# A pre-norm's variances and gain products placed on GpSimd, in a hybrid encoder layer on one core

## The chip, the core and the metric

The kernel runs on one core of a Trainium2 chip. A core has engines that each work through an instruction queue of their own, in order, and wait for each other by semaphores: TensorE (PE, with PEld for its weight loads), VectorE (DVE), ScalarE (ACT), GpSimd (POOL) and SyncE (SP, which here issues all the DMAs). SBUF is the on-chip memory of 128 partitions, PSUM the accumulators that PE writes. The metric is the device time of one execution in microseconds. Before the change it is 1018.42 us, the median of 3 runs (1018.4 to 1018.56).

## The reference

One layer over 1024 tokens of width 1024, all in float32. The input is normed, projected by one large matrix, and the parts of the projection go through three branches (causal pooling, short convolution, stick-breaking attention) whose gated results are projected, summed, projected again, normed and added to the input:

```python
def rms_norm(x, g):
    xf = x.astype(jnp.float32)
    y = xf * lax.rsqrt(jnp.mean(xf * xf, axis=-1, keepdims=True) + RMS_EPS)
    return (y * g.astype(jnp.float32)).astype(x.dtype)

def hybrid_layer(x, g_pre, w_in, pool_w, pool_scale, conv_w, conv_b, w_branch, w_out, g_post):
    h = rms_norm(x, g_pre)
    u = jnp.einsum('bsd,dn->bsn', h, w_in)
    ...
    return x + rms_norm(out, g_post)
```

Only the first line of the layer, the pre-norm h, concerns the change: per token the mean of the squares, plus RMS_EPS = 1e-6, to the power of -0.5, times the token's row, times g.

## The kernel before

**Precision and layout.** Every float32 operand of a matrix product is split into a high part (a rounded copy) and a low part (the rest), and each product is three products of PE: high by high, high by low, low by high. The high part is a cast on ACT, the low part a subtraction on DVE or POOL (`split`, lines 72 to 74: tiles w_hi, w_lo, q_w). The normed input is kept transposed, as hh (high) and hl (low): for each half of the model dimension (0 or 1, four blocks of 128 rows) and each half of the tokens (0 to 511, 512 to 1023). In the listings below, hh_0_70 and hl_0_74 belong to the first half of the tokens and half 0 of the model dimension, hh_0_72 and hl_0_76 to the first half of the tokens and half 1; hh_1_71 with hl_1_75 and hh_1_73 with hl_1_77 are the same two for the second half of the tokens.

**The pre-norm.** The tokens come in eight blocks of 128 (tile xt, 128 x 1024, eight buffers, loaded by line 267). `normed(i)` (lines 270 to 279) does for block i: on ACT the squares with their sum per token (tile ssq, line 274; a result row for the sum stands behind it as ACTIVATION_READ_ACCUMULATOR), on DVE the variance (tile var, line 276), on POOL its power of -0.5 (tile rstd, line 278), on DVE the product of row, rstd and g in place (line 279). g_bc is g, loaded once onto all partitions. `transposed(i)` (lines 281 to 291) then transposes the block on PE into a PSUM tile, four 128 x 128 pieces for each half of the model dimension, and splits it: ACT casts to hh (line 290), DVE subtracts to hl (line 291). The PSUM tiles xtp are four buffers, two for each block, so the transposes of a block reuse the buffers of the block two before it, once hh and hl of that block are written.

**The first products.** K and Q of the first head pair are computed while the norms go on (lines 319 to 326): for each half of the tokens, first K (three products for each of eight steps, `half_block`), then Q. In Q's first half the transposes of blocks 4 to 7 stand behind every second step. Each of the two results of K and Q sits in one of two PSUM banks (g_ps), and K's second half reuses the bank of K's first half, which `k_parts` (lines 237 to 248) empties: ACT copies it to khi (line 244), DVE subtracts to klo (line 245), ACT copies both to the other half of the partitions (lines 246 and 247), for two sides, one after the other. Q's weights (q_w) are split with their low part on POOL.

**What sets the order.** The program is written in a straight line, and the framework places instructions into the queues of the engines by its own estimate of when each is ready; so a moved instruction can change the order of its neighbours on every engine. SP's queue is not reordered by this change. The weights w_raw go through three buffers; a load into a buffer waits for the splits of the one before.

Of the kernel before, what the change touches and what calls it, by code (L numbers as in the profile page):

```python
# [11 lines left out]
ALU = mybir.AluOpType  # L12
# [3 lines left out]
D = 1024  # L16
# [5 lines left out]
EPS = 1e-6  # L22
# [13 lines left out]
def hybrid_block_kernel(ctx, tc, x, g_pre, w_in, pool_w, pool_scale, conv_w, conv_b, w_branch, w_out, g_post, out):  # L36
# [12 lines left out]
    nc = tc.nc  # L49
    op = lambda name, bufs, **kw: ctx.enter_context(tc.tile_pool(name=name, bufs=bufs, **kw))  # L50
# [210 lines left out]
    with tc.tile_pool(name="xp", bufs=1) as xp, tc.tile_pool(name="ps_s", bufs=2, space=PSUM) as ps_s:  # L261
        g_bc = xp.tile([P, D], F32, tag="g", name="g_bc")
# [7 lines left out]
        def normed(i):  # L270
            xt = xns[i]
            junk = xp.tile([P, D], F32, tag="junk", name="junk")
            ssq = xp.tile([P, 1], F32, tag="ssq", name="ssq", bufs=4)
            nc.scalar.activation(junk, xt, AF.Square, accum_out=ssq)
            var = xp.tile([P, 1], F32, tag="var", name="var", bufs=4)
            nc.vector.tensor_scalar(out=var, in0=ssq, scalar1=1.0 / D, scalar2=EPS, op0=ALU.mult, op1=ALU.add)
            r = xp.tile([P, 1], F32, tag="rstd", name="rstd", bufs=4)
            nc.gpsimd.tensor_tensor(out=r, in0=var, in1=expo[:, 0:1], op=ALU.pow)
            nc.vector.scalar_tensor_tensor(out=xt, in0=xt, scalar=r, in1=g_bc, op0=ALU.mult, op1=ALU.mult)

        def transposed(i):

# [16 lines left out]
        for i in range(2):  # L299
            normed(i)  # L300
# [3 lines left out]
        for i in range(2, 4):  # L304
            normed(i)
# [4 lines left out]
        for i in range(4, 8):  # L310
            normed(i)
# [25 lines left out]
    with tc.tile_pool(name="wt", bufs=3) as wtp, \  # L337
# [106 lines left out]
        for n in range(len(steps) + LAG + 1):  # L444
            if n < len(steps):
                p, s, i = steps[n]
# [371 lines left out]
    def square(ps, var):  # L818
        ssq = fin.tile([P, 1], F32, tag="ssq", name="ssq", bufs=4)
        nc.scalar.activation(junk[:, 0:ps.shape[-1]], ps, AF.Square, accum_out=ssq)  # L820
        o = fin.tile([P, 1], F32, tag="var", name="var", bufs=S // P + 4)
        if var is None:
            nc.vector.tensor_scalar(out=o, in0=ssq, scalar1=1.0 / D, scalar2=EPS, op0=ALU.mult, op1=ALU.add)
        else:
            nc.vector.scalar_tensor_tensor(out=o, in0=ssq, scalar=1.0 / D, in1=var, op0=ALU.mult, op1=ALU.add)
        return o
# [26 lines left out]
    for i in range(n_tok):  # L853
# [4 lines left out]
        var = kept_var[i]  # L858
        pieces = (slice(0, HALF),) if i < n_tok - 1 else (slice(0, 256), slice(256, HALF))
        for es in pieces:  # L860
            ps = out_bank()[:, 0:es.stop - es.start]
            out_products(i, ps, range(KB), 1, es)
            var = square(ps, var)
            scaled(ps, o1[:, es], slice(HALF + es.start, HALF + es.stop))
        r = fin.tile([P, 1], F32, tag="rstd", name="rstd", bufs=2)
# [45 lines left out]
```

## Time and profile before

| what | before |
|---|---|
| median of 3 runs | 1018.42 us |
| the profiled execution itself | 1018.75 us |
| its span, first to last instruction | 1017.0 us |
| mean granted TensorE clock | 0.994 |
| busy DVE / ACT / POOL | 632.2 / 447.2 / 448.3 us |
| end of block 3's sum of squares, start of its norm on DVE | 11.27, 16.46 us |

A line of the order of time reads: start and duration in us, engine, line of the kernel, operation, output<-inputs, shape, count, and in brackets how long the engine stood idle before it and what ended that. Groups and single lines of the program are given as durations in nanoseconds (min/median/max) with the start of the first and the last. The tables by stretch of time give, for each stretch, its length, then the busy time of PE, PEld, DVE, ACT and POOL with their counts, the granted TensorE clock (1.00 is full speed), the busy share of the DMA engines and what they moved in GB/s.

The profile in 40 equal slices shows where the pre-norm lies, in the first two slices of 25 us each:

```profile
PE   5999999999998999999999999999999999999997
...
POOL 3034443644565015445455554445555565655000
```

PE's first digit is 5: it waits for about half of the first slice. Behind that it is busy in nearly every slice.

### The profile page before, as it was taken

Reading aid. Unit: us, or ns where it says so; the run is one execution under the profiler, and the core shown is the slowest. Engines: PE = TensorE matmul, PEld = TensorE weight load, DVE = VectorE, ACT = ScalarE, POOL = GpSimd, SP = SyncE. Lnnn points to the kernel's source line nnn. Section 1 sums busy time; section 2 is a strip of 40 time slices with the busy share of each in tenths; the row PEclk is TensorE's granted clock in tenths of the full one; section 3 lists DMA queues with packets and bytes.
Section 4 is the critical chain, followed back from the end, with each engine's and each line's share of the span. In section 5 each row is a group of like instructions: output and inputs, shape, how many; then the busy total and the mean of one; then the engine's idle time right before and its main releaser. Section 6 shows DMA issues by size and latency. Waiting matters only on the chain.

```text
span 1017.0 us, 13273 instructions
## 1 busy us (share of the span) xinstructions
PE 989.9 (97%) x4752; PEld 829.1 (82%) x4752; DVE 632.2 (62%) x847; ACT 447.2 (44%) x871; POOL 448.3 (44%) x359
## 2 busy tenths in 40 slices
PE   5999999999998999999999999999999999999997
PEld 4788888888887888887888888888888888888886
DVE  6556776767776978899776776556333443464233
ACT  7557668658665553332222223343322422353111
POOL 3034443644565015445455554445555565655000
PEclk8999999999999999999999999999999999999999
DMA  6101000100101441222212224455433633166033
GB/s 240 51 22 33 31 22 22 42 21 22 32 23 32 165 156 62 92 75 68 80 61 68 79 72 164 150 195 175 135 124 124 217 121 111 61 201 222 1 125 125
DMA packets 43986, 97.09 MB, mean 95 GB/s; under 512 B 5264, under 2 KB 5520, under 8 KB 43920
## 3 DMA queue, kind: packets, MB, share of 16 engines
q1 hardware_dynamic: 43920, 96.24, 29.2%
q8 instruction: 38, 0.62, 0.3%
q14 instruction: 28, 0.23, 0.1%
HBM read 73.15 MB, written 23.07 MB: 95 GB/s over the span
## 4 chain that ended last, share of the span: by engine, by line
PE 89%; ACT 4%; DVE 3%; POOL 2%; issue 1%; DMA 1%; SPq 0%; POOLq 0%; DVEq 0%; ACTq 0%
PE q_ps L555 26%; PE g_ps L555 18%; PE g_ps L190 14%; PE pp L507 13%; PE o_ps L809 8%; PE o L434 3%; PE tp L420 2%; DVE sn L402 1%; PE z L398 1%; PE z L395 1%; ACT sn L399 1%; POOL sp L404 1%; POOL w_lo L74 1%; DMA g_bc<-in_pre_norm_g_dram 1%; ACT sp L400 1%
## 5 line engine op out<-in xcount | busy, mean ns | idle before, releaser
L74 POOL TENSOR_TENSOR w_lo<-s,w_hi 128x512 fp32r<-128x512 f32 x95 | 132.0, 1391 | 176.0 <-ACT w_hi L73 172.5
L404 POOL TENSOR_TENSOR sp<-sp,sn 128x127 f32<-128x127 f32 (+3 forms) x64 | 80.5, 1260 | 131.3 <-DVE sn L402 66.2
L74 POOL TENSOR_TENSOR w_lo<-s_raw,w_hi 128x512 fp32r<-128x512 f32 x70 | 94.9, 1355 | 93.3 <-ACT w_hi L73 89.6
L402 DVE TENSOR_TENSOR_SCAN sn<-sn,zeros 128x128 f32<-128x128 f32 (+3 forms) x64 | 101.9, 1592 | 46.3 <-ACT sn L399 41.6
L73 ACT CAST w_hi<-s 128x512 fp32r<-128x512 f32 x96 | 59.6, 621 | 131.4 <-PE q_ps L555 62.3
L190 PE MATMUL g_ps<-hh,w_hi 128*128 128x512 f32 x240 | 100.9, 420 | 0.3 <-ACT hh L290 0.3
L73 ACT CAST w_hi<-s_raw 128x512 fp32r<-128x512 f32 x70 | 43.5, 622 | 128.5 <-PE q_ps L555 62.2
L190 PE MATMUL g_ps<-hl,w_hi 128*128 128x512 f32 x240 | 95.2, 397 | 0.5 <-DVE hl L291 0.5
L190 PE MATMUL g_ps<-hh,w_lo 128*128 128x512 f32 x240 | 95.3, 397 | 0.0
L74 POOL TENSOR_TENSOR w_lo<-w_raw,w_hi 128x512 fp32r<-128x512 f32 x44 | 67.0, 1523 | 52.7 <-ACT w_hi L73 49.7
L555 PE MATMUL q_ps<-hh,w_lo 128*128 128x512 f32 x224 | 87.2, 389 | 0.7 <-POOL w_lo L74 0.7
L555 PE MATMUL q_ps<-hl,w_hi 128*128 128x512 f32 x224 | 87.2, 389 | 0.0
L555 PE MATMUL q_ps<-hh,w_hi 128*128 128x512 f32 x224 | 87.2, 389 | 0.0
L507 PE MATMUL pp<-yhi,w_lo 128*128 128x512 f32 x192 | 74.7, 389 | 0.0
L507 PE MATMUL pp<-ylo,w_hi 128*128 128x512 f32 x192 | 74.7, 389 | 0.0
L507 PE MATMUL pp<-yhi,w_hi 128*128 128x512 f32 x192 | 74.7, 389 | 0.0
L555 PE MATMUL g_ps<-hh,w_hi 128*128 128x512 f32 x160 | 62.3, 389 | 0.0
L555 PE MATMUL g_ps<-hl,w_hi 128*128 128x512 f32 x160 | 62.3, 389 | 0.0
L555 PE MATMUL g_ps<-hh,w_lo 128*128 128x512 f32 x160 | 62.2, 389 | 0.0
L399 ACT ACTIVATE sn<-z 128x384 f32<-128x384 f32 (+2 forms) x96 | 48.0, 500 | 28.3 <-PE z L398 17.8
L235 DVE TENSOR_TENSOR wl<-tp,wh 128x512 fp32r<-128x512 f32 (+2 forms) x96 | 50.2, 543 | 14.1 <-ACT wh L421 13.4
L421 ACT CAST wh<-tp 128x512 fp32r<-128x512 f32 (+2 forms) x96 | 44.9, 495 | 20.6 <-PE tp L420 15.2
(205 smaller groups left out, 2412.8 us busy)
## 6 DMA issues: line engine op xcount, KB each, us to landing
s_raw<-in_w_in_dram SPq DMA_DIRECT2D x96, 256.0 KB, 2.6
pr<-proj SPq DMA_DIRECT2D x48, 256.0 KB, 3.5
proj<-g SPq DMA_DIRECT2D x20, 512.0 KB, 3.0
w_raw<-in_w_in_dram SPq DMA_DIRECT2D x34, 256.0 KB, 2.6
w_raw<-in_w_branch_dram SPq DMA_DIRECT2D x24, 256.0 KB, 2.7
xt<-in_x_dram SPq DMA_DIRECT2D x8, 512.0 KB, 7.9
proj<-proj SPq DMA_DIRECT2D x8, 512.0 KB, 3.0
wo_raw<-in_w_out_dram SPq DMA_DIRECT2D x16, 256.0 KB, 3.2
```

What stands on the lines that cost most here:

```text
L73: nc.scalar.copy(hi, raw)
L74: eng.tensor_tensor(out=lo, in0=raw, in1=f32(hi), op=ALU.subtract)
L190: nc.tensor.matmul(ps, l[:, a], r[k // 4][t][:, k % 4, :], start=(n == 0), stop=(n == 3 * KB - 1))
L235: nc.vector.tensor_tensor(out=o, in0=a, in1=f32(b), op=ALU.subtract)
L399: nc.scalar.activation(sn[:, c0:c1], z[:, :w], AF.Sigmoid, scale=-0.125)
L402: nc.vector.tensor_tensor_scan(out=rev, data0=rev, data1=zeros.to_broadcast([P, n]), initial=1.0, op0=ALU.mult, op1=ALU.max)
L404: nc.gpsimd.tensor_tensor(out=sp[:, 0:n - 1], in0=sp[:, 0:n - 1], in1=sn[:, 1:n], op=ALU.mult)
L421: nc.scalar.copy(wh[c][:, 0:m, qsub], tp[:, 0:m, :])
L434: nc.tensor.matmul(o[:, cs], vc[:, j, s, :], wt[j // 4][:, j % 4, cs], start=(j == 0 and wt is wl), stop=(j == i and wt is wh))
L507: nc.tensor.matmul(pp, l[:, a], r[:, HALVES[t]], start=(n == 0), stop=(n == 3 * NB - 1))
L555: nc.tensor.matmul(bank, l[:, a], r[:, j, :], start=(n == 0), stop=(n == 11))
L809: nc.tensor.matmul(ps, l[:, a], r[:, es], start=(d == 0 and n == 0), stop=(d == KB - 1 and n == 2))
```

## The change

The variance of every block moves from DVE to POOL, right ahead of POOL's power. For the blocks 0 to 3 the product stays as it was. For the blocks 4 to 7 it becomes two instructions: POOL multiplies the raw row by g, in place, and DVE multiplies by rstd, a number for each token.

```diff
             var = xp.tile([P, 1], F32, tag="var", name="var", bufs=4)
-            nc.vector.tensor_scalar(out=var, in0=ssq, scalar1=1.0 / D, scalar2=EPS, op0=ALU.mult, op1=ALU.add)
+            nc.gpsimd.tensor_scalar(out=var, in0=ssq, scalar1=1.0 / D, scalar2=EPS, op0=ALU.mult, op1=ALU.add)
             r = xp.tile([P, 1], F32, tag="rstd", name="rstd", bufs=4)
             nc.gpsimd.tensor_tensor(out=r, in0=var, in1=expo[:, 0:1], op=ALU.pow)
-            nc.vector.scalar_tensor_tensor(out=xt, in0=xt, scalar=r, in1=g_bc, op0=ALU.mult, op1=ALU.mult)
+            if i < 4:
+                nc.vector.scalar_tensor_tensor(out=xt, in0=xt, scalar=r, in1=g_bc, op0=ALU.mult, op1=ALU.mult)
+            else:
+                nc.gpsimd.tensor_tensor(out=xt, in0=xt, in1=g_bc, op=ALU.mult)
+                nc.vector.tensor_scalar(out=xt, in0=xt, scalar1=r, scalar2=None, op0=ALU.mult)
```

Line numbers behind line 279 grow by four (L291 becomes L295). Past the first 45 us no queue changes its order.

POOL's queue before, from the last constant to the first weight split of the next stage:

```order
L170 AFFINE_SELECT future<-future 128x128
L278 TENSOR_TENSOR rstd<-var,expo 128x1 x6
L74 TENSOR_TENSOR q_w<-w_raw,q_w 128x512 x2
L278 TENSOR_TENSOR rstd<-var,expo 128x1 x2
L74 TENSOR_TENSOR w_lo<-w_raw,w_hi 128x512
```

The same place now, from block 5's variance on (block 4's three instructions stand ahead of it in the same order):

```order
L276 TENSOR_SCALAR var<-ssq 128x1
L282 TENSOR_TENSOR xt<-xt,g_bc 128x1024
L278 TENSOR_TENSOR rstd<-var,expo 128x1
L276 TENSOR_SCALAR var<-ssq 128x1
L282 TENSOR_TENSOR xt<-xt,g_bc 128x1024
L278 TENSOR_TENSOR rstd<-var,expo 128x1
L74 TENSOR_TENSOR q_w<-w_raw,q_w 128x512
L276 TENSOR_SCALAR var<-ssq 128x1
L282 TENSOR_TENSOR xt<-xt,g_bc 128x1024
L278 TENSOR_TENSOR rstd<-var,expo 128x1
L74 TENSOR_TENSOR q_w<-w_raw,q_w 128x512
L74 TENSOR_TENSOR w_lo<-w_raw,w_hi 128x512
```

The power of a block now stands behind that block's product, and the two splits of q_w, which stood ahead of the powers of blocks 6 and 7, stand on either side of block 7.

DVE's queue before, from the norm of block 5 to the splits of blocks 4 to 7 (hl_1):

```order
L279 SCALAR_TENSOR_TENSOR xt<-xt,rstd,g_bc 128x1024
L276 TENSOR_SCALAR var<-ssq 128x1 x2
L291 TENSOR_TENSOR hl_1_75<-xtp,hh_1_71 128x4x128
L279 SCALAR_TENSOR_TENSOR xt<-xt,rstd,g_bc 128x1024 x2
L74 TENSOR_TENSOR w_lo<-w_raw,w_hi 128x512
L235 TENSOR_TENSOR klo<-g_ps,khi 64x512 x2
L291 TENSOR_TENSOR hl_1_77<-xtp,hh_1_73 128x4x128
```

And now, from the four norms of blocks 0 to 3 to the same splits:

```order
L280 SCALAR_TENSOR_TENSOR xt<-xt,rstd,g_bc 128x1024 x4
L295 TENSOR_TENSOR hl_0_74<-xtp,hh_0_70 128x4x128 x2
L295 TENSOR_TENSOR hl_0_76<-xtp,hh_0_72 128x4x128 x2
L74 TENSOR_TENSOR w_lo<-w_raw,w_hi 128x512 x2
L295 TENSOR_TENSOR hl_0_74<-xtp,hh_0_70 128x4x128
L295 TENSOR_TENSOR hl_0_76<-xtp,hh_0_72 128x4x128
L295 TENSOR_TENSOR hl_0_74<-xtp,hh_0_70 128x4x128
L295 TENSOR_TENSOR hl_0_76<-xtp,hh_0_72 128x4x128
L283 TENSOR_SCALAR xt<-xt,rstd 128x1024 x4
L74 TENSOR_TENSOR w_lo<-w_raw,w_hi 128x512
L235 TENSOR_TENSOR klo<-g_ps,khi 64x512 x2
L295 TENSOR_TENSOR hl_1_75<-xtp,hh_1_71 128x4x128
```

The four scalings of blocks 4 to 7 now stand in one piece, behind all splits of blocks 0 to 3 and ahead of the weight split, both klo and the first split of block 4, which stood ahead of the norms of blocks 6 and 7. On ACT the squares of block 5 moved behind the four casts of blocks 2 and 3, and the casts of block 4 behind the first cast khi of line 246. On PE the first six transposes of block 4, which stood behind the first product of K, join the other two inside Q's first half.

## The prediction

> **What bounds the kernel now.** First the page: the share of each engine, and the chain that ended last.
>
> ```profile
> PE 989.9 (97%) x4752; PEld 829.1 (82%) x4752; DVE 632.2 (62%) x847; ACT 447.2 (44%) x871; POOL 448.3 (44%) x359
> ...
> PE 89%; ACT 4%; DVE 3%; POOL 2%; issue 1%; DMA 1%; SPq 0%; POOLq 0%; DVEq 0%; ACTq 0%
> ```
>
> PE is busy for 97% and carries 89% of the chain, so the pre-norm can cost or save only what PE waits for it, and PE's work behind it follows back to back: a shift of PE's start is a shift of the end. Next, the order of time on PE for the first 40 us, where the pre-norm lies (tile xtp: transposes of normed tokens; g_ps: the products of the first K and Q blocks).
>
> ```profile
> 17.89 1.94 PE L288 MATMUL xtp<-ident,xt 128*128 128x128 f32 x8 [3.14 <-DVE xt L279]
> ...
> 21.73 0.78 PE L190 MATMUL g_ps<-hl,w_hi 128*128 128x512 f32 x1
> ...
> 33.57 1.03 PE L288 MATMUL xtp<-ident,xt 128*128 128x128 f32 x8
> ...
> 38.11 0.50 PE L190 MATMUL g_ps<-hl,w_hi 128*128 128x512 f32 x1 [0.47 <-DVE hl L291]
> ...
> 38.11 15.07 PE g_ps L190 x65
> ```
>
> Two gates count. **Gate 1**: tokens 0 to 511 are split and the products run from 21.73. **Gate 2**: tokens 512 to 1023 are split and the products of the second half run from 38.11; by the last row, from the chain in order of time, PE then runs 15.07 us without a wait. What the change does to the end is what it does to gate 2. The rows of ACT and DVE ahead of it:
>
> ```profile
> 28.53 0.58 ACT L244 CAST khi<-g_ps 64x512 fp32r<-64x512 f32 x1 [5.00 <-PE g_ps L190]
> 29.86 0.58 ACT L246 CAST khi<-g_ps 64x512 fp32r<-64x512 f32 x1 [0.75 <-DVE klo L235]
> ...
> 31.58 1.08 ACT L290 CAST hh<-xtp 128x512 fp32r<-128x512 f32 x2
> ...
> 36.03 0.58 ACT L257 CAST qa<-g_ps 64x512 fp32r<-64x512 f32 x1 [0.55 <-PE g_ps L190]
> ...
> 25.74 2.48 DVE L279 SCALAR_TENSOR_TENSOR xt<-xt,rstd,g_bc 128x1024 f32<-128x1024 f32 x2 [2.01 <-POOL rstd L278]
> 28.14 0.68 DVE L74 TENSOR_TENSOR w_lo<-w_raw,w_hi 128x512 fp32r<-128x512 f32 x1
> 29.14 0.68 DVE L235 TENSOR_TENSOR klo<-g_ps,khi 64x512 fp32r<-64x512 f32 x1 [0.32 <-ACT khi L244]
> ```
>
> The last two norms, one weight split and the first klo stand in that order on DVE. ACT's second khi waits for that klo, and the casts hh of blocks 4 to 7 queue on ACT behind it. From klo's start to gate 2 it takes 38.11 - 29.14 = 8.97 us.
>
> **The change, part by part.**
>
> *Removed from DVE*: eight variances and, for blocks 4 to 7, the product of three operands. *Added*: a one-input instruction of DVE there, and on POOL eight variances and four products of 128x1024. The prices (duration rows give min/median/max in ns):
>
> ```profile
> L276 DVE TENSOR_SCALAR var<-ssq x8: 143/146/154, 5.7 to 22.8; 128x1 f32<-128x1 f32 x8
> ...
> L279 DVE SCALAR_TENSOR_TENSOR xt<-xt,rstd,g_bc x8: 1276/1284/1286, 7.6 to 26.9; 128x1024 f32<-128x1024 f32 x8
> ...
> L643 DVE TENSOR_SCALAR pb<-pb,convw_sb,convb_sb x4: 814/816/816, 477.7 to 591.9; 128x1024 f32<-128x1024 f32 x4
> ...
> L278 POOL TENSOR_TENSOR rstd<-var,expo x8: 542/548/552, 5.9 to 25.7; 128x1 f32<-128x1 f32 x8
> ...
> L149 POOL MEMSET expo<- x1: 101/101/101, 0.7 to 0.7; 128x4 f32 x1
> ...
> L374 POOL TENSOR_TENSOR ysb<-ysb,tmp x3: 2402/2402/4384, 199.8 to 307.2; 128x1024 f32<-128x1024 f32 x3
> ...
> L404 POOL TENSOR_TENSOR sp<-sp,sn 128x1023 f32<-128x1023 f32 x8 | 16.0, 1998 | 9.3 <-DVE sn L402 4.8 <-PE z L398 4.6
> ...
> L74 POOL TENSOR_TENSOR q_w<-w_raw,q_w x2: 1282/1576/1871, 22.1 to 23.9; 128x512 fp32r<-128x512 f32 x2
> ```
>
> Product on POOL: 2.40, from L374, the same operation, shape and in-place form; one column less and not in step (L404) took 2.00, the low end. Scaling on DVE: 0.82, from L643, one input of that shape. A variance on POOL is shown nowhere; it lies between the memset (0.10) and the power (0.55), and I take 0.20, nearer to the memset, which like it reads no second tensor. So a block from 4 on costs POOL 0.20 + 2.40 + 0.55 = 3.15 us, against 0.55 before.
>
> *Gate 1.*
>
> ```profile
> 11.09 0.18 ACT L274 ACTIVATION_READ_ACCUMULATOR junk<-xt 128x1 f32 x1
> ...
> 15.65 0.14 DVE L276 TENSOR_SCALAR var<-ssq 128x1 f32<-128x1 f32 x1
> ...
> 16.46 1.28 DVE L279 SCALAR_TENSOR_TENSOR xt<-xt,rstd,g_bc 128x1024 f32<-128x1024 f32 x1
> ...
> 34.54 1.89 DVE L291 TENSOR_TENSOR hl<-xtp,hh 128x512 fp32r<-128x512 f32 x3 [0.94 <-ACT hh L290]
> ```
>
> Block 3's sum of squares ends at 11.27, but DVE reaches its variance only at 15.65; POOL would do it near 11.5, and DVE would norm block 3 at 12.1 to 13.2 instead of at 16.46. By the new order the split of block 3 stands ninth behind it (eight instructions from 13.3 at 0.60, as the last row spaces them): ready at 18.8, gate 1 at about 18.9, 2.9 earlier. Against this, the product of block 4 can get in the way of DVE's two weight splits, which now stand in that row, and hold them for 2.4 us: gate 1 then at 21.3. I take 21.3; it hardly matters, because gate 2 comes from POOL, as follows.
>
> *POOL's row up to gate 2.* DVE scales blocks 4, 5, 6 and 7 one behind the other, and the weight split, both klo and all splits of blocks 4 to 7 now stand behind the scaling of block 7. That waits for POOL's last power, and POOL must first do:
>
> ```profile
> 15.27 1.06 ACT L274 ACTIVATE junk<-xt 128x1024 f32<-128x1024 f32 x1
> ...
> 19.86 0.59 ACT L290 CAST hh<-xtp 128x512 fp32r<-128x512 f32 x1 [0.27 <-PE xtp L288]
> ```
>
> - Block 4: ACT squares it some 0.8 earlier than at 15.27, two casts now behind it; variance at 15.6, product to 18.3, power to 18.8.
> - Block 5: on ACT four casts of blocks 2 and 3 now precede its square, which wait for transposes. Before, they ended at 20.4 with block 3 late; with block 3 early they end near 19.2, and the square gives its sum at 20.4 (20.0 to 20.9).
> - Blocks 5, 6, 7 and the first split of q_w, which stands between them: 3 x 3.15 + 1.28 = 10.73, to 31.1.
> - Waits at the SBUF port that POOL and DVE share:
>
> ```profile
> 307.16 2.40 POOL L374 TENSOR_TENSOR ysb<-ysb,tmp 128x1024 f32<-128x1024 f32 x1
> ...
> 249.21 2.02 DVE L402 TENSOR_TENSOR_SCAN sn<-sn,zeros 128x896 f32<-128x896 f32 x1 [0.87 <-ACT sn L399]
> 307.94 3.51 DVE L402 TENSOR_TENSOR_SCAN sn<-sn,zeros 128x896 f32<-128x896 f32 x1 [0.92 <-ACT sn L399]
> ...
> 477.70 0.82 DVE L643 TENSOR_SCALAR pb<-pb,convw_sb,convb_sb 128x1024 f32<-128x1024 f32 x1
> ...
> 478.02 1.64 POOL L74 TENSOR_TENSOR w_lo<-s,w_hi 128x512 fp32r<-128x512 f32 x1 [1.44 <-ACT w_hi L73]
> ```
>
> A scan of 2.02 took 3.51 when POOL's product had started first, that is, it began when the product was done; and POOL's split, 1.28 alone, took 1.64 behind a DVE instruction of just the new form. So each scaling of blocks 4, 5 and 6 holds POOL for 0 to 0.82: 0 to 2.46 in all, and no row says how often. I take the middle, 1.2: the last power ends at **32.3** (bounds 20.0 + 10.73 = 30.7, or 29.5 with products of 2.00, and 20.9 + 10.73 + 2.46 = 34.1).
>
> *From there to gate 2.* POOL's own next instruction, the second split of q_w, starts at once and has the port first (1.28), then the scaling (0.82), the weight split (0.60 to the next start): klo at **35.0**, against 29.14: **+5.9** (bounds: no wait, 30.7 + 1.42 = 32.1, +3.0, or +1.8 with products of 2.00; all, 34.1 + 2.70 = 36.8, +7.7). Behind klo the 8.97 us stay: ACT has one cast hh more there (0.5), and loses a wait for PE of about that length.
>
> *The clock.* PE has finished six of eight steps of Q's first half near 34.5 (the second split of q_w lands at 33.6) and then waits for a bank of xtp, which the first split of block 4 frees: 2.44 from klo to the first hh (29.14 to 31.58), then cast, split and a hop, 3.9 in all, so at 38.9. Such a wait was here once:
>
> ```profile
> 317.43 0.44 PE L420 MATMUL tp<-ident,sp 128*128 128x128 f32 x2 [2.86 <-DVE wl L235]
> ...
> 316.00:317.40 1.40, 0.00 (x0) 0.00 (x0) 1.40 (x3) 0.98 (x3) 0.44 (x1) 1.00 0.00 0
> 317.40:319.00 1.60, 1.57 (x6) 1.34 (x7) 1.53 (x4) 0.37 (x1) 1.55 (x1) 0.70 0.00 0
> 320.00:321.00 1.00, 1.00 (x6) 1.00 (x5) 0.56 (x2) 0.00 (x0) 0.00 (x0) 0.50 0.00 0
> 321.00:322.00 1.00, 1.00 (x7) 0.91 (x6) 0.30 (x1) 0.59 (x1) 0.00 (x0) 0.78 0.00 0
> ```
>
> After 2.86 us of idling the granted clock (third number from the right) fell to 0.50 for about 3.5 us. A wait of 4 us should do the same: 1.75 lost, less what PE waits for ACT there anyway (0.7): **+1.1** (0 to 1.75).
>
> **Sum**: 5.9 + 1.1 = 7.0 on the span of 1017.0, which is 1025.75 against the profiled run's 1018.75; that run was 0.33 above the median of 1018.42, so **1025.4**.
>
> One rule bears on the middle value. The Trainium skill (SBUF — State Buffer, Who interferes with whom) has the shared port as an exclusive lock, held by whoever comes first for the whole instruction. The two rows above agree for long instructions (1.49 and 0.36 of waiting); that POOL's variance and power wait as well, no run here shows. By it every scaling stands in POOL's way, and the sum would be rival B's. The skill's VectorE: DVE Perf Modes (Mode 2×_2P) doubles the rate of a one-input fp32 instruction out of SBUF; L643 shows 0.82 against 1.28, less than that, and the row decides.
>
> **Rivals.**
> - *A, no waits at the port.* Products and scalings happen to miss each other: +3.0, the wait of PE short enough for the clock: 1021.4 (1020.2 with products of 2.00). Against it: every scaling starts just where POOL wants its next block.
> - *B, every small instruction waits too.* Last power at 34.1, +7.7, clock +1.1: 1027.2. A POOL variance as dear as the power (0.35 more for each of three on that row) or scalings no faster than 1.28 end there as well.
> - *C, the chain on POOL stays hidden, and gate 1's gain is kept.* It decides at the last power: klo is not held if that ends by 29.14 - 1.42 = 27.7, which needs 3.0 us less than the bound of 30.7, products of about 1.4 instead of 2.40. The gain is then up to 2.9: 1015.5 to 1018.4. For it: POOL has no other urgent work there; against: the shortest near row has 2.00. Half way there, the time stays within 0.2%.
>
> **How the numbers follow.** Forecast 0.55, A 0.13, B 0.20, C 0.12. Under 0.2% (2.04 us, about what a measurement can tell) either way: 0.08, all from C and the edge of A; faster 0.04; slower 0.88. The range goes from 1020.8, between A's two prices, to 1028.3, B with the dearest clock and a dearer variance; about 0.2 is left out, most of it C.
>
> **What would show it.** DVE's four scalings as the last instructions before klo, klo near 35, idle of PE of 3 to 4 us ahead of the transposes of block 6 put down to DVE's split, clock 0.5 behind it, gate 2 near 45 and everything behind it unchanged. POOL products well over 2.40 with DVE working beside them confirm the port. Wrong if products run near 1.4, if klo starts before 31, or if gate 2 is late and the end is not.

## The result and the profile after

The changed kernel is slower by 0.7%: 1026.01 us, the median of 4 runs (1024.92 to 1027.73), against 1018.41 of the kernel before in the same rounds; the ratio is 1.0071, with a 95% interval of 1.0059 to 1.0084. The profiled execution was the slowest of the four, 1027.73 us with a span of 1025.5. A second measurement, among the experiments below, gave 1025.49 us (1024.93 to 1026.65, ratio 1.0067, interval 1.0055 to 1.008).

The page first, PE's busy time and the chain that ended last:

```profile
PE 992.1 (97%) x4752; PEld 830.0 (81%) x4752; DVE 633.1 (62%) x839; ACT 447.6 (44%) x871; POOL 461.0 (45%) x371
...
PE 84%; ACT 4%; DVE 4%; POOL 4%; issue 3%; DMA 1%; SPq 0%; POOLq 0%; DVEq 0%; ACTq 0%
```

PE's share of the chain went from 89% to 84%, and POOL's from 2% to 4%. That is 5% of the span, some 50 us, while the span grew by 8.5. Another execution of the same kernel has 87%, and a variant below whose time cannot be told from that of the kernel before has 85%. So nothing is read from these shares; the gates decide. The rows in order of time that answer to those of before, on PE, ACT and DVE (the last of PE's is from the chain):

```profile
21.44 0.50 PE L190 MATMUL g_ps<-hl,w_hi 128*128 128x512 f32 x1 [2.34 <-DVE hl L295]
...
38.45 1.97 PE L292 MATMUL xtp<-ident,xt 128*128 128x128 f32 x8 [3.72 <-DVE hl L295]
...
45.13 0.50 PE L190 MATMUL g_ps<-hl,w_hi 128*128 128x512 f32 x1 [0.23 <-DVE hl L295]
...
45.13 15.04 PE g_ps L190 x65
...
35.26 0.58 ACT L246 CAST khi<-g_ps 64x512 fp32r<-64x512 f32 x1 [7.68 <-DVE klo L235]
...
27.48 1.74 DVE L283 TENSOR_SCALAR xt<-xt,rstd 128x1024 f32<-128x1024 f32 x1 [2.79 <-POOL rstd L278]
32.27 1.76 DVE L283 TENSOR_SCALAR xt<-xt,rstd 128x1024 f32<-128x1024 f32 x1 [3.04 <-POOL rstd L278]
33.95 0.68 DVE L74 TENSOR_TENSOR w_lo<-w_raw,w_hi 128x512 fp32r<-128x512 f32 x1
34.55 0.67 DVE L235 TENSOR_TENSOR klo<-g_ps,khi 64x512 fp32r<-64x512 f32 x1
```

Gate 1 is at 21.44, nearly where it was (21.73). DVE then stands 2.79 and 3.04 us until POOL's powers of blocks 6 and 7 are there, klo comes at 34.55 instead of 29.14, ACT's second khi has waited 7.68 us for it, and PE has waited 3.72 us for a bank of xtp. Gate 2 is at 45.13 instead of 38.11, and PE's work behind it again runs 15 us without a wait. POOL's rows between 11 and 34 us show what DVE waited for:

```profile
11.78 0.91 POOL L276 TENSOR_SCALAR var<-ssq 128x1 f32<-128x1 f32 x1 [0.46 <-ACT junk L274]
...
18.40 0.99 POOL L278 TENSOR_TENSOR rstd<-var,expo 128x1 f32<-128x1 f32 x1
20.24 0.19 POOL L276 TENSOR_SCALAR var<-ssq 128x1 f32<-128x1 f32 x1 [0.85 <-DVE hl L295]
20.52 2.40 POOL L282 TENSOR_TENSOR xt<-xt,g_bc 128x1024 f32<-128x1024 f32 x1
22.86 1.01 POOL L278 TENSOR_TENSOR rstd<-var,expo 128x1 f32<-128x1 f32 x1
...
24.23 2.71 POOL L282 TENSOR_TENSOR xt<-xt,g_bc 128x1024 f32<-128x1024 f32 x1
26.90 0.55 POOL L278 TENSOR_TENSOR rstd<-var,expo 128x1 f32<-128x1 f32 x1
27.41 1.26 POOL L74 TENSOR_TENSOR q_w<-w_raw,q_w 128x512 fp32r<-128x512 f32 x1
28.76 0.51 POOL L276 TENSOR_SCALAR var<-ssq 128x1 f32<-128x1 f32 x1
29.35 2.37 POOL L282 TENSOR_TENSOR xt<-xt,g_bc 128x1024 f32<-128x1024 f32 x1
31.68 0.55 POOL L278 TENSOR_TENSOR rstd<-var,expo 128x1 f32<-128x1 f32 x1
32.20 1.28 POOL L74 TENSOR_TENSOR q_w<-w_raw,q_w 128x512 fp32r<-128x512 f32 x1
```

From block 5's variance at 20.24 POOL is never idle: three products, three powers, two more variances, one split of q_w, until the last power ends at 32.23. The groups of the four new or moved kinds of instruction (min/median/max in ns):

```profile
L276 POOL TENSOR_SCALAR var<-ssq x8: 192/192/909, 6.0 to 28.8; 128x1 f32<-128x1 f32 x8
L278 POOL TENSOR_TENSOR rstd<-var,expo x8: 549/552/1009, 7.6 to 31.7; 128x1 f32<-128x1 f32 x8
L282 POOL TENSOR_TENSOR xt<-xt,g_bc x4: 2366/2387/2713, 16.1 to 29.4; 128x1024 f32<-128x1024 f32 x4
L283 DVE TENSOR_SCALAR xt<-xt,rstd x4: 785/1650/1757, 21.9 to 32.3; 128x1024 f32<-128x1024 f32 x4
```

Undisturbed, a variance takes 0.19, a power 0.55, a product 2.37 and a scaling 0.79. The medians and maxima above that are waits between POOL and DVE. The row starts when ACT has the sum of squares of block 5, at 20.15:

```profile
19.96 0.19 ACT L274 ACTIVATION_READ_ACCUMULATOR junk<-xt 128x1 f32 x1
```

### The profile page after: what moved, and what is told of

Its sections match the earlier page's. It is cut to its first block, busy times and chain, and to the rows that moved or that the text cites. A ratio compares the mean times of both kernels' runs of the same rounds, so it can differ in the third digit from the quotient of the medians.

```text
span 1025.5 us, 13273 instructions
## 1 busy us (share of the span) xinstructions
PE 992.1 (97%) x4752; PEld 830.0 (81%) x4752; DVE 633.1 (62%) x839; ACT 447.6 (44%) x871; POOL 461.0 (45%) x371
## 4 chain that ended last, share of the span: by engine, by line
PE 84%; ACT 4%; DVE 4%; POOL 4%; issue 3%; DMA 1%; SPq 0%; POOLq 0%; DVEq 0%; ACTq 0%
PE q_ps L559 26%; PE g_ps L559 17%; PE pp L511 13%; PE g_ps L190 12%; PE o_ps L813 8%; PE o L438 3%; PE tp L424 2%; DVE sn L406 2%; POOL sp L408 1%; PE z L402 1%; POOL w_lo L74 1%; PE z L399 1%; ACT sn L403 1%; DMA xt<-in_x_dram 1%; ACT sp L404 1%
## 5 line engine op out<-in xcount | busy, mean ns | idle before, releaser
L133 DVE TENSOR_TENSOR s<-s_raw 128x512 f32<-128x512 f32 x48 | 41.5, 864 | 22.4 <-POOL w_lo L74 21.9
```

The lines of the kernel that those rows point to most:

```text
L133: nc.vector.tensor_tensor(out=o, in0=a, in1=b, op=how)
```

## The experiments

The theory: POOL's row of products, small instructions and splits up to its last power holds DVE's first klo, and with it gate 2; the end moves by what gate 2 moves. The rivals: the new order on DVE or the moved variances are the cost, and not the products; or the cost arises later in the program. The changed kernel and the twelve runs made after it in one table: gate 2 as the profiles show it, its distance from 38.11, the ratio of the times with its interval, and the difference of the medians in the same rounds.

| kernel | gate 2 | shift | ratio [95%] | median less before's |
|---|---|---|---|---|
| changed kernel | 45.13 | +7.02 | 1.0071 [1.0059, 1.0084] | +7.60 |
| the same again | 44.26 | +6.15 | 1.0067 [1.0055, 1.0080] | +6.67 |
| PE kept busy in its wait | 44.77 | +6.66 | 1.0052 [1.0038, 1.0065] | +5.92 |
| product on POOL for blocks 6, 7 only | 44.36 | +6.25 | 1.0061 [1.0047, 1.0075] | +6.03 |
| scaling on ACT | 44.27 | +6.16 | 1.0057 [1.0042, 1.0073] | +5.80 |
| products alone, variances on DVE | 42.82 | +4.71 | 1.0045 [1.0032, 1.0059] | +4.46 |
| changed kernel, q_w split on DVE | 42.18 | +4.07 | 1.0048 [1.0034, 1.0063] | +4.63 |
| product over half the columns | 42.09 | +3.98 | 1.0032 [1.0022, 1.0043] | +3.30 |
| variances alone | 40.10 | +1.99 | 1.0008 [0.9999, 1.0017] | +1.59 |
| variances of blocks 0 to 3 alone | 39.07 | +0.96 | 1.0008 [0.9999, 1.0017] | +0.77 |
| product and scaling both on DVE | 38.89 | +0.78 | 1.0008 [0.9999, 1.0017] | +0.79 |
| variances alone, q_w split on DVE | 37.79 | -0.32 | 1.0000 [0.9991, 1.0009] | -0.44 |
| variance of block 3 alone | 37.32 | -0.79 | 0.9997 [0.9988, 1.0006] | -0.33 |

Over a spread of nearly 8 us the time follows gate 2 within 0.8 us. So nothing of weight has to be looked for behind it, and the question is what moves gate 2. One caution: gate 2 is that of one profiled execution, and in the kernels whose first four variances are on POOL block 4's sum of squares was ready at anything from 15.49 to 16.64, depending on when the tokens arrived. That much of a shift belongs to the execution and not to the kernel; the medians carry less of it.

### Variances alone on GpSimd

```diff
-            if i < 4:
-                nc.vector.scalar_tensor_tensor(out=xt, in0=xt, scalar=r, in1=g_bc, op0=ALU.mult, op1=ALU.mult)
-            else:
-                nc.gpsimd.tensor_tensor(out=xt, in0=xt, in1=g_bc, op=ALU.mult)
-                nc.vector.tensor_scalar(out=xt, in0=xt, scalar1=r, scalar2=None, op0=ALU.mult)
+            nc.vector.scalar_tensor_tensor(out=xt, in0=xt, scalar=r, in1=g_bc, op0=ALU.mult, op1=ALU.mult)
```

> Variances on GpSimd for all eight blocks, the norm of every block still one three-operand instruction of VectorE. Theory (the four products of 2.4 us on POOL, in a row up to its last power, hold VectorE's first klo and with it gate 2): without them POOL's last power is over before 26, the first klo is not held and starts at 26 to 27.5, gate 1 is at 18.9 to 19.5, gate 2 at 35.2 to 36, and the time is 1015.5 us (1015 to 1016.5). Rival (moving the variances to POOL, or the order in which VectorE's four norms now stand in one piece ahead of klo, is what costs, and the products matter little): gate 2 stays at 43 to 45 and the time at 1024 or more.

Measured 1020.55 us (11 runs, 1018.72 to 1021.54; before 1018.96), gate 2 at 40.10. The products are most of the loss, as the theory has it; but the gain of about 3 us that it put beside them is not there, and that was a miss. Two rows of DVE and two of POOL in the order of time say why:

```profile
24.91 2.30 DVE L279 SCALAR_TENSOR_TENSOR xt<-xt,rstd,g_bc 128x1024 f32<-128x1024 f32 x1 [0.72 <-POOL rstd L278]
27.93 2.29 DVE L279 SCALAR_TENSOR_TENSOR xt<-xt,rstd,g_bc 128x1024 f32<-128x1024 f32 x1 [0.72 <-POOL rstd L278]
```

```profile
24.85 1.29 POOL L74 TENSOR_TENSOR q_w<-w_raw,q_w 128x512 fp32r<-128x512 f32 x1
...
27.86 1.28 POOL L74 TENSOR_TENSOR q_w<-w_raw,q_w 128x512 fp32r<-128x512 f32 x1
```

The norms of blocks 6 and 7 take 2.30 and 2.29 instead of 1.28: each became ready 0.06 or 0.07 us after POOL had begun a split of q_w, and was held for 1.0. klo came at 30.75. About 0.6 of that belongs to the execution: block 4's sum of squares was ready at 16.34, in the changed kernel at 15.72.

### The same, with q_w's splits on VectorE

```diff
-            split(raw, q_w[:, 0, ks], q_w[:, 1, ks], nc.gpsimd)
+            split(raw, q_w[:, 0, ks], q_w[:, 1, ks], nc.vector)
```

> The kernel with all variances on GpSimd and the norm as before on VectorE (e1_var_only), and the two subtractions that split q_w on VectorE too, so that POOL has nothing but 128x1 instructions there. Theory (in that kernel VectorE's norms of blocks 6 and 7 took 2.30 instead of 1.28 because POOL's splits of q_w had the port, and that is what ate the gain of gate 1): all norms take 1.28, klo starts at 27.8 to 28.8 instead of 30.75 though VectorE has 1.2 us more work ahead of it, gate 2 at 37 to 38.3, 1017.5 to 1019.2 us. Rival (VectorE's order, with all norms ahead of klo, ate it): klo at 30.5 or later, since two more instructions stand ahead of it, and gate 2 at 40 or later.

The norms, the splits and klo in DVE's order of time:

```profile
23.88 1.28 DVE L279 SCALAR_TENSOR_TENSOR xt<-xt,rstd,g_bc 128x1024 f32<-128x1024 f32 x1 [0.44 <-POOL rstd L278]
25.88 1.28 DVE L279 SCALAR_TENSOR_TENSOR xt<-xt,rstd,g_bc 128x1024 f32<-128x1024 f32 x1 [0.72 <-POOL rstd L278]
27.08 1.28 DVE L74 TENSOR_TENSOR q_w<-w_raw,q_w 128x512 fp32r<-128x512 f32 x2
28.29 0.68 DVE L235 TENSOR_TENSOR klo<-g_ps,khi 64x512 fp32r<-64x512 f32 x1
```

All norms take 1.28, and gate 2 falls from 40.10 to 37.79. klo comes 2.5 us earlier, 0.6 of it because the tokens arrived earlier. Ahead of klo stand two more instructions, the splits, and one less, the weight split, which the new order puts behind it; so DVE has 0.6 us more to do there. The port theory (what POOL runs holds DVE, since both use one port of SBUF) is borne out, and the rival by order falls. The experiment doesn't separate the splits' holding of the norms from the time they took in POOL's own row, where block 7's variance stood behind one of them. The time, 1018.38 us against 1018.82, cannot be told from that of the kernel before.

### Variances of blocks 0 to 3 alone, and of block 3 alone

```diff
-            nc.vector.tensor_scalar(out=var, in0=ssq, scalar1=1.0 / D, scalar2=EPS, op0=ALU.mult, op1=ALU.add)
+            eng = nc.gpsimd if i < 4 else nc.vector      # in the second kernel: if i == 3
+            eng.tensor_scalar(out=var, in0=ssq, scalar1=1.0 / D, scalar2=EPS, op0=ALU.mult, op1=ALU.add)
```

> The kernel before with the variances of blocks 0 to 3 alone on GpSimd; nothing else is changed. Theory (what is good in the change is that block 3's variance no longer waits behind VectorE's splits; what costs is that the powers of blocks 5 to 7 then come late on POOL, behind waits at the port): gate 1 at 20 to 20.8, klo at 28 to 30, gate 2 at 36.8 to 38.8, 1017 to 1019.5 us, the best of the variants. Rival (any earlier gate 1 is eaten by VectorE's norms standing in one piece ahead of klo): klo at 30.5 or later, gate 2 at 39.5 or later, 1020 or more.

> The kernel before with block 3's variance alone on GpSimd; VectorE's order stays as it was but for that one instruction and block 3's norm, which moves ahead of one split. Theory (the good part of the change is that one instruction): gate 1 is 0.6 to 0.9 earlier, klo, which follows PE's first product, as well, gate 2 at 37.2 to 37.6, 0.5 to 0.9 us less in all, which five rounds may not tell from none. Rival (a later wait takes it up): gate 2 at 38 or later.

With blocks 0 to 3 gate 1 is at 20.05, klo at 29.72, gate 2 at 39.07 and the time 1019.38 against 1018.61: no gain, with klo and the time where the first side expected them and gate 2 between the two. DVE's norms and splits and POOL's powers and q_w splits held each other up there too: the two splits of q_w took 4.19 together, and DVE's weight split between two norms 1.70 instead of 0.68. With block 3 alone gate 1 did not move, 21.68 against 21.73, which neither side expected; gate 2 came at 37.32 all the same. PE's rows of that kernel:

```profile
20.51 1.51 PE L289 MATMUL xtp<-ident,xt 128*128 128x128 f32 x6 [0.28 <-DVE xt L280]
...
21.68 0.78 PE L190 MATMUL g_ps<-hl,w_hi 128*128 128x512 f32 x1
```

In this order of PE transposes of block 4 stand ahead of the first hl product, so gate 1 follows block 4's norm there, not block 3's; the 0.8 us came from PE's clock, which was back at full speed about 1.5 us sooner (a product of gate 1 takes 0.40 from 22.98 on, before 0.41 from 24.44 on). When the clock comes back differs from run to run, as shown below, so this is no gain that one can count on.

### Products alone, variances on VectorE

```diff
-            nc.gpsimd.tensor_scalar(out=var, in0=ssq, scalar1=1.0 / D, scalar2=EPS, op0=ALU.mult, op1=ALU.add)
+            nc.vector.tensor_scalar(out=var, in0=ssq, scalar1=1.0 / D, scalar2=EPS, op0=ALU.mult, op1=ALU.add)
```

> The other half of the change alone: variances stay on VectorE as before, blocks 4 to 7 get the product on GpSimd and the scaling on VectorE. Theory (POOL's row of products up to its last power sets gate 2; variances and small waits are a lesser part): gate 2 at 43 to 44.5 and 1023 to 1025.5 us, with gate 1 no earlier than before (21.7 or later, since a scaling now stands ahead of block 3's split). Rival (the variances on POOL, waiting at the port and ordering VectorE anew, carry about half or more of the loss): gate 2 at or below 41.5 and 1021.5 or less.

1023.07 us against 1018.61, gate 2 at 42.82: the products alone carry about two thirds of the loss. They also reach into the first half of the tokens, where gate 1 came at 25.72; block 3's norm on DVE and the products of blocks 4 and 5 on POOL:

```profile
17.52 3.38 DVE L280 SCALAR_TENSOR_TENSOR xt<-xt,rstd,g_bc 128x1024 f32<-128x1024 f32 x1
...
17.46 5.65 POOL L282 TENSOR_TENSOR xt<-xt,g_bc 128x1024 f32<-128x1024 f32 x2
```

The norm took 3.38 instead of 1.28, because the product of block 4 had begun 0.06 us earlier, at 17.46.

### The product over half the columns

```diff
-                nc.gpsimd.tensor_tensor(out=xt, in0=xt, in1=g_bc, op=ALU.mult)
+                nc.gpsimd.tensor_tensor(out=xt[:, 0:HALF], in0=xt[:, 0:HALF], in1=g_bc[:, 0:HALF], op=ALU.mult)
```

> The changed kernel with the product with g on GpSimd over the first 512 of 1024 columns only (the factor g is left out of the other half for blocks 4 to 7); every instruction and its place stays. Theory (length of POOL's serial row): a product takes 1.2 to 1.3, so the last power ends 3.6 to 4.7 earlier, at 27.5 to 28.6, klo starts at 29.8 to 31.2, TensorE's wait for the transposes of block 6 is too short for the clock to fall, gate 2 at 39 to 40.5, time 1019 to 1020.5. Rival (the place of the scalings ahead of klo, or the number of instructions, not the length of the products): gate 2 at 44 or later, 1025.

A product took 1.28 (the group of four by lines, with busy time and mean):

```profile
L282 POOL TENSOR_TENSOR xt<-xt,g_bc 128x512 f32<-128x512 f32 x4 | 5.1, 1284 | 0.3
```

POOL's last power ended at 29.63 instead of 32.23, klo came at 31.95 instead of 34.55, and the time was 1022.26 against 1018.96: less than half of the loss is left, with every instruction in its place. So it is the length of the row, not the order, that carries at least half. The gain was smaller than the theory had it, because block 5's variance came 0.45 later there, and because the clock did fall just behind PE's wait of 2.93 us (0.63 in the stretch from 36 to 37, 0.50 after it): from klo to gate 2 it was 10.14.

### The product on GpSimd for blocks 6 and 7 only

```diff
-            if i < 4:
+            if i < 6:
```

> The changed kernel with the product on GpSimd for blocks 6 and 7 alone; blocks 4 and 5 keep VectorE's three-operand norm. First theory (each product on POOL has its price in gate 2, so two of four cost half of what four cost beyond the kernel with the variances alone, whose gate 2 was at 40.1): gate 2 at 42 to 42.8, 1022 to 1023. Second theory (POOL's row is bound by when ACT has squared a block: products 4 and 5 run while POOL would wait for squares 5 and 6, and only those of 6 and 7 with their waits are on the path): gate 2 at 43.8 to 45 and 1024 to 1026, nearly as with four.

1024.64 us against 1018.61, gate 2 at 44.36, 10.68 behind klo: the second theory. Two of the four products cost nearly as much as all four. POOL's row there:

```profile
20.81 1.41 POOL L278 TENSOR_TENSOR rstd<-var,expo 128x1 f32<-128x1 f32 x1
22.30 1.29 POOL L276 TENSOR_SCALAR var<-ssq 128x1 f32<-128x1 f32 x1
23.67 2.39 POOL L282 TENSOR_TENSOR xt<-xt,g_bc 128x1024 f32<-128x1024 f32 x1
```

Block 6's product starts at 23.67, with all four it was 24.23. One reason is that of the theory: block 6's sum of squares is not there before 21.67. The other was not thought of: without products 4 and 5 DVE does its norms of 1.28 again, and for those POOL's power of block 5 and variance of block 6 stood 0.86 and 1.10 us.

### The scaling on ACT

```diff
-                nc.vector.tensor_scalar(out=xt, in0=xt, scalar1=r, scalar2=None, op0=ALU.mult)
+                nc.scalar.activation(xt, xt, AF.Copy, scale=r)
```

> The changed kernel with the scaling by one number per token on ACT instead of VectorE. Theory (POOL's small instructions waited for VectorE's scalings and norms at the shared port): with no scaling on VectorE the powers of blocks 5 to 7 take 0.55 each (before 1.01, 0.55, 0.55), the variances of blocks 5 to 7 take 0.19 each (the last took 0.51), and products stay at 2.37 to 2.40 (one took 2.71). Gate 2 gains little, since ACT's squares now queue behind scalings that wait for POOL: 43.5 to 45.5, 1024 to 1026.5. Rival (POOL's small instructions are slow for a reason of POOL's own, such as right behind a long instruction): powers behind a product still take 0.9 to 1.0.

POOL's small instructions behind long ones, in the order of time:

```profile
24.59 0.55 POOL L278 TENSOR_TENSOR rstd<-var,expo 128x1 f32<-128x1 f32 x1
...
29.11 0.55 POOL L278 TENSOR_TENSOR rstd<-var,expo 128x1 f32<-128x1 f32 x1
29.74 0.19 POOL L276 TENSOR_SCALAR var<-ssq 128x1 f32<-128x1 f32 x1
...
32.35 0.55 POOL L278 TENSOR_TENSOR rstd<-var,expo 128x1 f32<-128x1 f32 x1
```

With no scaling on DVE nothing of blocks 5 to 7 waits: the powers take 0.55, the variances 0.19, the products 2.38 to 2.41. Only block 4's power, behind DVE's weight split, still takes 1.00. So the excess in the changed kernel (1.01, 2.71, 0.51) is waiting for DVE, not something of POOL's own. The time hardly changed, 1024.41 us against 1018.61, since now ACT's squares queue behind scalings that wait for POOL.

### Both steps on VectorE

```diff
-                nc.gpsimd.tensor_tensor(out=xt, in0=xt, in1=g_bc, op=ALU.mult)
+                nc.vector.tensor_tensor(out=xt, in0=xt, in1=g_bc, op=ALU.mult)
```

> The changed kernel with the product with g for blocks 4 to 7 as a two-operand instruction of VectorE instead of GpSimd; VectorE then works two instructions (about 1.28 + 0.8) where before it worked one. Theory (POOL's products are the cost, not VectorE's work): POOL's last power is early, VectorE has about 3.2 us more than the kernel before but gains some 2.9 at gate 1; klo at 27.5 to 30, gate 2 at 36.5 to 39, 1017 to 1019.5. Rival (two instructions and four scalings in one piece ahead of klo are the cost wherever they run): 1023 or more.

1019.75 us against 1018.96, gate 2 at 38.89. Twice the instructions and about 4 us more work on DVE cost 0.08% (at most 0.17% by the interval); the products cost what they do because they stand in POOL's row. klo came at 30.73, 0.7 later than the theory allowed: each pair of scalings took 2.44, where 1.5 would do, beside a split of q_w on POOL. In this execution the tokens also arrived 0.9 later than in the changed kernel's (block 4's sum of squares at 16.64).

### PE kept busy in its wait

```diff
+                        if n == 5:
+                            warm = ps_s.tile([P, HALF], F32, tag="warm", name="warm", bufs=1)
+                            for m in range(16):
+                                nc.tensor.matmul(warm, ws[1][1][:, 0:P], hl[1][0][:, 3, :], start=(m == 0), stop=(m == 15))
                         transposed(4 + n // 2)
```

> The changed kernel with 16 extra matmuls of 128x512 into a bank of PSUM that nobody reads, put on TensorE just ahead of the transposes of block 6, where it idles from 34.6 to 38.45; their result is not used. Theory (the idle of 3.7 us costs 1.1 us more through the granted clock, and the runs of the changed kernel differ by 2.8 us because of how long clock stays low): the clock stays at 1.00 between 36 and 44, gate 2 comes at 44.0 instead of 45.13, the time is 1024.9 us or less and the runs lie within 0.6 of each other. Rival (the clock costs nothing that is not hidden, the scatter has its cause later in the program): gate 2 at 45.1, 1026, with the same scatter. Second rival: the clock is the cause at gate 2 alone, and the scatter stays.

The clock stayed at 1.00. In this execution the pre-norm ran some 0.8 later from the arrival of the tokens on (klo 0.86 later, at 35.41), and gate 2 came at 44.77: 9.36 after klo, where the changed kernel took 10.58. The median was 1024.88 us (1024.01 to 1026.51; before 1018.96). The interval of its ratio, 1.0038 to 1.0065, overlaps with those of the changed kernel, so a gain in time is not shown; what is shown is the distance from klo to gate 2. The runs still lie 2.5 us apart, so the second rival holds for the scatter.

### The changed kernel again

> The changed kernel unaltered, beside the two below. In eight variants the time moved by what gate 2 moved, within 0.8 us; the changed kernel's first profile had gate 2 at +7.0 and its median +7.6. If gate 2 is all there is: gate 2 at +6.7 to +7.1 and the median 6.2 to 7.4 above that of the kernel before in these rounds. Rival (something later in the program adds 0.6 to 1.5): the median 7.6 or more above, with gate 2 at +7.0.

Median 1025.49 against 1018.82, +6.67: no cost is left to be found behind gate 2. The profile had gate 2 at +6.15, earlier than either side expected, although klo stood at 34.65, where the first profile has it (34.55). The tables by stretch show the difference (third number from the right is the granted clock); first the changed kernel's first profile, then its second:

```profile
36.00:37.00 1.00, 0.00 (x0) 0.00 (x0) 0.02 (x1) 0.96 (x3) 0.00 (x0) 0.83 0.68 231
37.00:38.00 1.00, 0.00 (x0) 0.00 (x0) 0.97 (x2) 1.00 (x2) 0.00 (x0) 0.50 0.04 16
...
43.00:44.00 1.00, 1.00 (x8) 0.93 (x7) 0.37 (x1) 0.81 (x2) 0.00 (x0) 0.75 0.00 0
```

```profile
39.00:40.00 1.00, 1.00 (x8) 0.82 (x7) 0.09 (x1) 0.98 (x3) 0.00 (x0) 1.00 0.00 0
40.00:41.00 1.00, 1.00 (x5) 0.77 (x4) 0.98 (x2) 1.00 (x3) 0.00 (x0) 0.54 0.00 0
...
43.00:44.00 1.00, 1.00 (x5) 0.50 (x3) 0.82 (x2) 0.77 (x2) 0.00 (x0) 0.75 0.00 0
```

PE's wait is nearly the same, 3.72 and 3.43 us, but the clock fell at about 36.7 in the one and at about 40 in the other, when PE had been at work again for 1.5 us; both times it was back before 44. From klo to gate 2 it was 10.58 us in the one and 9.61 in the other. The same happened at the wait of 2.87 us behind 320: in the first profile the clock was low from about 323.4 to 330.2, in the second from 323.4 to 326.8, and what lay 0.92 apart ahead of it lay 2.2 apart behind it. So 2.2 of the 2.8 us between these two executions of one kernel come at two stretches of low clock. The other 0.6 comes at 823 in the first profile: a load of y landed about 1 us later there, ACT's cast of it and POOL's weight split behind it came late (821.28; in the second profile 818.03, 3.25 earlier instead of 2.2), and PE stood for that split. What lay 2.20 apart ahead of this place lies 2.80 apart behind it.

### The changed kernel with q_w's splits on VectorE

The edit is that of the other kernel with these splits on VectorE, made to the changed kernel.

> The changed kernel with the two subtractions that split q_w on VectorE instead of GpSimd. The forecast had two terms for them, 1.28 in POOL's row between blocks 6 and 7 and 1.28 ahead of the last scaling at the port. Theory (both terms are real): POOL's last power ends at 30.4 to 31.4 instead of 32.23, VectorE's last scaling takes 0.8 instead of 1.76, klo starts at 31.8 to 33, gate 2 at 42.3 to 43.6, and the time is 1.4 to 2.6 us less than the changed kernel's, 1023 to 1024.5. Rival (the splits only filled gaps, the products alone set the row): klo at 34 or later, and the time within 0.7 us of the changed kernel's.

```profile
31.55 0.75 DVE L283 TENSOR_SCALAR xt<-xt,rstd 128x1024 f32<-128x1024 f32 x1 [0.44 <-POOL rstd L278]
...
32.83 0.68 DVE L235 TENSOR_TENSOR klo<-g_ps,khi 64x512 fp32r<-64x512 f32 x1
```

The last scaling takes 0.75 instead of 1.76, klo comes 1.7 earlier. PE's wait is then 1.25, the clock stays at 1.00, and gate 2 is at 42.18. So the splits do cost; of the 1.28 ahead of the last scaling 1.0 is there. Of the other term, 1.28 in POOL's row, nothing shows. POOL's last power ended at 31.52 instead of 32.23, but the row had also begun 0.7 earlier, with block 5's sum of squares at 19.44 (0.2 of that by the arrival of the tokens; the rest was not settled). The row is 12.08 long in both kernels: without the splits on POOL, block 7's variance (0.75) waited for a scaling, and its product (2.73) and power (1.00) waited for the splits on DVE. The time is 1023.83 us, 4.63 above the kernel before, where the changed kernel was 7.60 and 6.67 above it: 2.0 to 3.0 less.

## Why the prediction was right, point by point

Predicted 1025.4, measured 1026.01 and, a second time, 1025.49. The shift of gate 2, forecast +7.0, was +7.02 and +6.15. Step by step:

- *Gate 2 sets the end.* Held in all thirteen rows of the table, within 0.8 us. The first profile's further 1.5 us came behind it: about 1.25 at the low clock behind 323, which lasted 3.4 us longer than before the change, and 0.6 at the late load at 823, less 0.35 ahead of both. The forecast had nothing for that, and in the second profile it was not there.
- *Gate 1 at 21.3.* Measured 21.44, but by two errors that cancel. Block 3's norm was put at 12.1 and came at 13.36, because its variance on POOL (0.91 instead of 0.19) stood behind the norm of block 2 on DVE; and the hold of DVE's weight splits, put at 2.4, was 1.35 (2.63 instead of 1.28). The 18.9 without a hold was too early for the same reason: with the variances alone gate 1 was at 20.73.
- *Prices.* Variance 0.20 against 0.19, product 2.40 against 2.37 to 2.40, power 0.55, scaling 0.82 against 0.79. Right.
- *The row from block 5's sum of squares.* Put at 20.4, measured 20.15. Three blocks and one split, 10.73 and 1.2 of waits; measured 12.08 to 32.23, of which waits are 0.46 (power 5), 0.34 (product 6) and 0.32 (variance 7), 1.12 in all. The middle value was right, and that was partly luck, since it stood halfway between two bounds and no row of the kernel before gave it. The mechanism is rival B's: the small instructions do wait, two of the three waits being theirs. Each scaling meets one instruction of POOL's, and for only a part of its length, since POOL's turns and DVE's interlock: more often the scaling waited (1.56, 1.74 and 1.76 instead of 0.79). That is why B's sum of 1027.2 did not come with B's mechanism. The Trainium skill (SBUF — State Buffer, Who interferes with whom) has the lock for whole instructions and leaves none out for being small; rows 11.78, 18.40, 22.86 and 28.76 agree (0.91 and 0.51 instead of 0.19, 0.99 and 1.01 instead of 0.55).
- *What of the row is on the path.* Here the working was right in sum and not in its parts. That product 5 counts in full was not so: products 4 and 5 taken away brought 0.8 us of gate 2 against the first profile and nothing against the second, not 3.15 or more, partly because what DVE does in their place holds POOL as well.
- *From the last power to klo.* Put at 2.70, measured 2.32: the scaling, 1.76 with its wait and 0.79 alone, was held for 1.0 by q_w's split, not for its whole 1.28, which had begun at 32.20, just ahead of the power's end.
- *From klo to gate 2.* 8.97 + 1.1 of clock, 10.07; measured 10.58 and 9.61. With the clock held it was 9.36, and 9.35 in three other variants with this order on ACT whose clock stayed at 1.00 (variances alone, those of blocks 0 to 3 alone, q_w split on DVE). So the path that was taken to stay at 8.97 is 0.4 longer, and the clock cost 1.2 in one execution and 0.25 in the other: inside the bounds of 0 to 1.75, but not one number.
- *The sum.* +7.02 in the first profile is +5.41 to klo, where 5.9 was forecast, and +1.61 from there, where 1.1 was; the second has +5.51 and +0.64. The path is as forecast, but that the sum came out to the second digit is two misses of half a microsecond that cancel.
- *Rivals.* A (no waits) fell with the row; C (POOL hidden) was far off, the last power at 32.23 against 27.7. Rival B's condition was met and its price was not.

What rival C put beside hidden products, and the first experiment expected with more confidence, a gate-1 gain of up to 2.9 that reaches the end, no kernel showed: neither the variances alone nor any of their parts beat the kernel before by more than the measurement can tell.

## What to carry to other kernels

Before work goes to an idle engine, write out that engine's row up to the instruction that others wait for, from the moment its last input is ready; the sum of that row, not the engine's share of busy time, is the price. Work it out again from each later input: what POOL does while it would wait for its next input anyway costs little (products 4 and 5, 0.8 us of gate 2 at most). Where DVE and POOL share a port, count every instruction of either, small ones too, as able to stand for the whole of the other's instruction, and look for the long ones that have nothing to do with the change (here q_w's splits, whose place was worth 2 to 3 us). A wait of PE of 3 to 4 us costs its own length and, in the four cases here (waits of 2.93 to 3.72 us), a low clock worth 0.25 to 1.3 us, going by how much longer than 9.35 it took from klo to gate 2; so differences under 0.3% between kernels with such waits need several runs.

## What the runs showed of the hardware that was not expected

- An instruction of 128x1 on POOL waits until DVE's instruction is done: 0.91 instead of 0.19, 1.01 instead of 0.55, up to 1.29 for a variance that came right behind the start of a norm of 1.28. DVE's splits with one operand in PSUM were not held: four of them took 2.47 beside the product from 20.52, as they do alone.
- The clock fell around waits of PE of 2.86, 2.93, 3.43 and 3.72 us and did not fall after 1.25, 2.17 and 2.50. The length of one wait does not decide it alone: with the scaling on ACT it fell at about 36.45 although no wait there was over 2.05 (2.05 before 34.19 and 0.64 before 36.01). Nor is the moment fixed: in the changed kernel's first profile it fell 1.9 us into the wait, in the second 1.5 us after PE had gone back to work. The Trainium skill (TensorE: Matmul & The Clock Gate, Part 1: The HAM clock gate) has a free-running window of about 3.4 us that decides. The differing moments of the fall after the same wait agree with a window that runs on its own; that a wait of 2.86 is enough, or one of 2.05 with a short one behind it, goes beyond its rule of a whole idle window.
